# A 3x3 convolution with max pooling on one core: seven weight blocks turned by three transposes each, with a copied first tap, in a new program order

## The chip, the core and the metric

One core of a Trainium2 chip runs the whole kernel. The metric is the device time of one execution in microseconds (us); the time of a version is the median of several executions.

The engines: PE (TensorE) multiplies, PEld is its weight load, DVE (VectorE) and ACT (ScalarE) do element-wise work, POOL (GpSimd) does element-wise work and issues the converting loads, and SP (SyncE) issues the other transfers. Each engine works through a queue of its own in program order and waits at an instruction until the results it needs are there.

## The reference

```python
batch, c_in, h, w, c_out, k = 16, 64, 64, 64, 128, 3
x_pad = np.pad(x, ((0, 0), (0, 0), (1, 1), (1, 1)), mode='constant')
conv[b, co] += weight[co, ci, kh, kw] * x_pad[b, ci, kh:kh+h, kw:kw+w]   # over b, co, ci, kh, kw
output[b, c, i, j] = np.max(conv[b, c, 2*i:2*i+2, 2*j:2*j+2])
```

A convolution of 16 images with 64 channels of 64 x 64 to 128 channels, padded by one, and then the maximum over 2 x 2 squares. All of it is float32 on the outside; the kernel multiplies in bfloat16.

## The kernel before

**Tiles.** Two images lie together on the 128 partitions: image 0 of the pair on partitions 0 to 63, image 1 on 64 to 127. There are 8 pairs, each cut into 4 strips of 16 image rows, so 32 strips, numbered 0 to 31. A strip gives 8 rows of the output, and for each half h (image) two results of 8 x 64 numbers, one PSUM bank each: A for the odd and B for the even row of each pooled pair.

**Products.** A product (`product`, line 227) is three matmuls, one for each horizontal tap kw, on the 64 partitions of one image. The matmuls of h = 0 and h = 1 use different row halves of PE and are put into two lanes; the program takes one product from each lane and writes their matmuls in turn (lines 251 to 255). The text below calls this a pair. Strips of type "K" use the products PA1, PA2 into A and PB1, PB2 into B, straight from the image rows, and PR into B after a row maximum. Strips of type "W" use sums, differences and skip differences of neighbouring rows: P2, whose result is copied from A to B (`seed`, SE), P0 into A, P3 and P1 into B. In strip 0 the products are cut into halves a and b of four rows each.

**Weight blocks.** There are seven: G0, G1, G2 (the rows of the filter), D0 = G0 - G1, D2 = G2 - G1, GM and GP (half of G0 + G2 minus or plus G1; GS is the sum G0 + G2). Each is first made as `wq[m]`, 128 output channels on the partitions and 64 input channels for each tap along the row (`wcast` on ACT or `wpair` on DVE). Then PE turns it (`turn`, line 146): each transpose takes two neighbouring taps, 128 columns, so that one tap comes to the lower 64 partitions and the next one to the upper 64. `turn_out` (line 155) copies the turned block from PSUM to `wt[m]`. For h = 0 a matmul reads the lower half, for h = 1 the upper half (`tap_of`, line 135).

A block that isn't in `RING` (line 44) has its three taps between two slots of zeros (line 129) and needs four transposes. A block in `RING` has its three taps first and a copy of tap 0 behind them (`ring`, line 138, on POOL), and needs three.

**Row work.** Image rows 0 to 64 of pair 0 and 0 to 33 of pair 1 come as float32 through SP (line 89, six transfers) and are converted by `cast_rows` (CA on ACT, CV on DVE, line 100); all later rows are loaded and converted by transfers that POOL issues (`cload`, LK, line 94). `rows_op` (line 258) makes sums (S), differences (E) and skip differences (D): plain letters and a J run on DVE, a g on POOL. After the products: `evac` (EV, ACT) copies A out, `rowmax` (MX, DVE, line 294) takes the maximum of A and B into B, `odd` (OD, ACT, line 303) copies the odd columns, `colmax` (CM, DVE, line 316) takes the maximum with the even ones, and `store` follows on SP.

**Order.** The program order is written out by hand as a list of tokens, `ORDER` (line 326). Each token is one call; a number behind @ is the PSUM bank that the call takes. The queue of each engine is this list, cut down to the tokens of that engine. For example `uGM TGM@4` copies the first tap of GM, then turns the block into bank 4, and `VvGM` copies it out on DVE. Eight matmuls on constants (line 385) run before the list.

Of the kernel before, what the change touches and what calls it, by code (L numbers as in the profile page):

```python
# [10 lines left out]
def kernel(  # L11
# [123 lines left out]
    def tap_of(m, kw, h):  # L135
        return (kw - h) % K if m in RING or m == "GN" and "GM" in RING else kw + 1 - h

    def ring(m):
        behind_vector(nc.gpsimd.tensor_copy(out=wq[m][:, K, :], in_=wq[m][:, 0, :]))
# [173 lines left out]
    def colmax(part, s, h):  # L313
# [18 lines left out]
        EV.2.1 EV.1.0 MX.2.1 SE.1.1@4 PB1.2.0@2 LK.1.33.64.1 LK.2.0.33 Sg.3 MX.1.0 EV.2.0 OD.0.1 P0.1.1 P3.1.1
        CA.1.17.33 PR.2.1 EV.1.1 CM.0.1 OD.0.0 PB2.2.0 P2.3.0@7 EJ.4 P1.1.0 P2.3.1@3 SE.3.0@0 MX.1.1 OD.1.0
        OD.2.1 P1.1.1 P2.4.1@6 CM.0.0 Dg.5 LK.2.33.64 P0.3.0 LK.3.0.33 CM.1.0 SE.3.1@1 MX.2.0 P3.3.0 CM.2.1
        P0.3.1 PR.2.0 P3.3.1 OD.1.1 EV.3.0 SE.4.1@5 EV.3.1 P2.5.0@7 SE.5.0@3 CM.1.1 P2.4.0@4 D.4 P0.4.1 P0.5.0
        SJ.4 OD.2.0 LK.3.33.64 EV.4.1 MX.3.1 P3.4.1 MX.3.0 P2.5.1@6 P1.3.1 Dg.7 LK.4.0.33 CM.2.0 P3.5.0 EV.5.0
        SE.4.0@2 P1.3.0 SE.5.1@7 MX.4.1 LK.4.33.64 P1.4.1 P0.5.1 MX.5.0 P3.5.1 OD.3.0 P0.4.0 OD.3.1 EV.4.0 EJ.6
        OD.4.1 P3.4.0 CM.3.0 EV.5.1 P1.5.0 Dg.6 CM.3.1 MX.4.0 OD.5.0 P2.6.1@4 PA1.8.1@1 CM.4.1 P2.7.0@0 P1.4.0
        CM.5.0 SE.7.0@6 PA1.8.0@3 OD.4.0 SE.6.1@5 MX.5.1 PA2.8.1 EV.8.1 P0.7.0 P1.5.1 D.9 SJ.6 CM.4.0 P0.6.1
        OD.5.1 EV.7.0 LK.5.0.33 P3.7.0 PA2.8.0 P2.7.1@1 EV.6.1 P2.6.0@2 PB1.8.0@4 D.11 E.9 PB2.8.0 P3.6.1 CM.5.1  # L340
        SE.7.1@0 EJ.10 MX.6.1 EJ.12 EV.8.0 P0.7.1 SE.6.0@7 P2.9.1@3 EV.7.1 P1.6.1 P0.6.0 P3.7.1 P3.6.0 SE.9.1@1
        P0.9.1 OD.6.1 P2.11.1@2 LK.5.33.64 Sg.8 MX.7.0 P1.7.0 EV.6.0 MX.8.0 PR.8.0 CM.6.1 P3.9.1 MX.6.0 MX.7.1
        OD.7.0 P2.9.0@5 P1.7.1 EV.9.1 Dg.10 Sg.9 P1.6.0 OD.8.0 CM.7.0 CM.8.0 MX.9.1 SE.11.1@3 SE.9.0@6 P2.11.0@4
        OD.6.0 P0.11.1 CM.6.0 SJ.10 EJ.16 P3.11.1 OD.7.1 P0.9.0 EV.11.1 MX.11.1 CM.7.1 P2.10.1@2 Dg.12 SE.11.0@7
        P3.9.0 P1.9.1 P1.11.1 P0.11.0 EV.9.0 P3.11.0 MX.9.0 SE.10.1@5 P0.10.1 OD.9.1 PB1.8.1@1 CM.9.1 P2.12.0@0
        P1.9.0 P2.10.0@4 EV.11.0 P3.10.1 MX.11.0 OD.11.1 PB2.8.1 EV.10.1 OD.9.0 D.15 CM.11.1 SE.12.0@2 CM.9.0
        P1.11.0 SE.10.0@3 Dg.13 MX.10.1 P0.12.0 P2.12.1@6 OD.11.0 P0.10.0 P3.12.0 P1.10.1 EV.12.0 CM.11.0
        P3.10.0 SE.12.1@7 MX.8.1 P2.13.1@0 OD.10.1 P0.12.1 EV.10.0 P3.12.1 SJ.12 SE.13.1@4 CM.10.1 MX.12.0
        P0.13.1 P2.16.0@5 Dg.16 MX.10.0 EV.12.1 P1.12.0 SE.16.0@6 P3.13.1 PR.8.1 P1.10.0 OD.12.0 MX.12.1 CM.12.0
        OD.10.0 P0.16.0 CM.10.0 P1.12.1 EV.13.1 PA1.14.1@0 PA2.14.1 P2.13.0@2 PA1.14.0@3 OD.8.1 PA2.14.0 EV.16.0  # L350
        MX.13.1 SE.13.0@5 OD.12.1 P3.16.0 P0.13.0 Eg.15 Sg.15 CM.8.1 SJ.16 D.17 CM.12.1 P2.17.1@1 P1.13.1
        EV.14.0 EV.14.1 P2.15.0@7 SE.17.1@3 P2.15.1@0 P0.17.1 P3.17.1 OD.13.1 EV.13.0 SJ.18 P3.13.0 MX.16.0
        P1.16.0 PB1.14.1@4 SE.15.0@2 CM.13.1 P0.15.0 P3.15.0 EV.17.1 OD.16.0 SE.15.1@1 EJ.18 S.14 PB2.14.1
        MX.13.0 CM.16.0 P1.13.0 P0.15.1 EV.15.0 MX.17.1 PB1.14.0@6 P2.17.0@7 MX.15.0 MX.14.1 LK.6.0.33 OD.13.0
        P1.17.1 P3.15.1 CM.13.0 OD.17.1 EV.15.1 P1.15.0 SE.17.0@5 Dg.21 Sg.21 Dg.18 CM.17.1 MX.15.1 PB2.14.0
        PR.14.1 P2.16.1@0 OD.15.0 OD.14.1 Eg.21 CM.15.0 SE.16.1@3 MX.14.0 P1.15.1 P0.17.0 EV.17.0 P2.18.1@2
        OD.15.1 P3.17.0 CM.14.1 P0.16.1 PR.14.0 MX.17.0 SE.18.1@4 CM.15.1 EV.16.1 OD.14.0 P3.16.1 P2.18.0@7 D.19
        MX.16.1 LK.6.33.64 P1.17.0 P0.18.1 SE.18.0@1 P2.19.0@0 CM.14.0 P3.18.1 EV.18.1 OD.17.0 P0.18.0 P1.16.1
        LK.7.0.33 Dg.22 MX.18.1 CM.17.0 SE.19.0@6 P3.18.0 P2.21.1@2 P0.19.0 EV.18.0 P1.18.1 P2.19.1@7 MX.18.0
        OD.16.1 SE.21.1@5 P0.21.1 EJ.24 CM.16.1 P3.19.0 P1.18.0 EV.19.0 OD.18.1 SE.19.1@0 P3.21.1 Dg.25 P0.19.1  # L360
        LK.7.33.64 MX.19.0 EV.21.1 P2.21.0@3 OD.18.0 SE.21.0@2 P1.19.0 CM.18.1 EV.19.1 OD.19.0 PA1.20.0@4
# [98 lines left out]
```

## Time and profile before

| what | value |
|---|---|
| median of 3 runs | 103.37 us (102.65 to 103.5) |
| the profiled execution | 102.83 us, span 101.1 us, mean granted clock 0.994 |
| busy: PE, DVE, ACT, POOL | 94.8, 88.6, 85.4, 60.7 us |
| first product on PE | at 6.99 us of the span |
| moved by the transfers | 18.81 MB |

The span runs from the first to the last instruction; the profiled execution's time holds 1.7 us besides. In a row of the timeline stand the start, the duration from the first start to the last end of a merged group, the engine, the line, the operation and its shapes; behind a bracket, how long the engine was idle before it and what ended that. Rows of the chain are the stretches of work that led to the end, one after the other.

### The profile page before, as it was taken

Reading aid. Unit: us, or ns where it says so; the run is one execution under the profiler, and the core shown is the slowest. Engines: PE = TensorE matmul, PEld = TensorE weight load, DVE = VectorE, ACT = ScalarE, POOL = GpSimd, SP = SyncE. Lnnn points to the kernel's source line nnn. Section 1 sums busy time; section 2 is a strip of 40 time slices with the busy share of each in tenths; the row PEclk is TensorE's granted clock in tenths of the full one; section 3 lists DMA queues with packets and bytes.
Section 4 is the critical chain, followed back from the end, with each engine's and each line's share of the span. In section 5 each row is a group of like instructions: output and inputs, shape, how many; then the busy total and the mean of one; then the engine's idle time right before and its main releaser. Section 6 shows DMA issues by size and latency. Waiting matters only on the chain.

```text
span 101.1 us, 2423 instructions
## 1 busy us (share of the span) xinstructions
PE 94.8 (94%) x861; PEld 57.0 (56%) x861; DVE 88.6 (88%) x177; ACT 85.4 (85%) x188; POOL 60.7 (60%) x64
## 2 busy tenths in 40 slices
PE   6969999999999999999999999999999999999930
PEld 2349455548655656666666666676665555545300
DVE  0588999999999999999999999999976998969870
ACT  5540999999898999999988999899599989999830
POOL 7233486999606946798069995865994489600000
PEclk9999999999999999999999999999999999999997
DMA  2999649999999999993895159999925207332143
GB/s 74 270 359 412 266 47 178 195 237 221 226 230 228 229 232 225 304 334 135 98 192 182 62 65 218 206 264 218 292 99 179 73 6 242 122 113 98 52 150 109
DMA packets 11740, 18.81 MB, mean 186 GB/s; under 512 B 976, under 2 KB 9168, under 8 KB 11728
## 3 DMA queue, kind: packets, MB, share of 16 engines
q0 software_dynamic: 1872, 6.80, 36.6%
q1 hardware_dynamic: 9856, 11.87, 36.1%
q8 instruction: 6, 0.10, 0.4%
q14 instruction: 6, 0.05, 0.2%
HBM read 17.07 MB, written 8.39 MB: 252 GB/s over the span
## 4 chain that ended last, share of the span: by engine, by line
PE 79%; ACT 7%; DMA 5%; DVE 5%; issue 0%; SPq 0%; DVEq 0%
PE acc L242 78%; DMA xf<-in_x_dram 5%; ACT xb L100 3%; DVE xb L100 1%; DVE xf L316 1%; ACT acc L281 1%; ACT ev L289 1%; ACT od L303 1%; ACT ev L287 1%; DVE skip L272 1%; PE acc L149 0%; DVE dif L272 0%; SPq L106 0%; DVE wt_GP L161 0%; DVE sum L272 0%
## 5 line engine op out<-in xcount | busy, mean ns | idle before, releaser
L242 PE MATMUL acc<-skip,wt_G 64*128 64x504 bf16 (+1 forms) x312 | 65.7, 377 | 0.1
L242 PEld LDWEIGHTS <-wt_G 64*128 64x128 bf16 x432 | 34.8, 94 | 19.2 <-issue 2.6
L294 DVE TENSOR_TENSOR acc<-acc,ev 128x512 f32<-128x512 f32 x64 | 43.1, 693 | 2.0 <-ACT ev L287 1.5
L272 POOL TENSOR_TENSOR skip<-xb 128x1024 bf16<-128x1024 bf16 x17 | 36.0, 2126 | 11.0 <-DVE sum L272 4.6
L242 PE MATMUL acc<-dif,wt_GM 64*128 64x512 bf16 (+1 forms) x156 | 38.7, 376 | 0.0
L242 PE MATMUL acc<-sum,wt_GP 64*128 64x512 bf16 (+1 forms) x156 | 38.0, 377 | 0.2 <-DVE acc L294 0.2
L287 ACT ACTIVATE ev<-acc 128x512 f32<-128x512 f32 x52 | 31.3, 606 | 1.1 <-PE acc L242 0.8
L281 ACT COPY acc<-acc 128x512 f32<-128x512 f32 x52 | 30.5, 591 | 1.4 <-DVE xf L316 0.4
L303 ACT COPY od<-acc 128x256 f32<-128x256 f32 x64 | 23.3, 380 | 3.1 <-PE acc L242 2.8
L272 POOL TENSOR_TENSOR sum<-xb 128x512 bf16<-128x512 bf16 x10 | 11.5, 1150 | 12.3 <-DVE dif L272 4.5
L242 PEld LDWEIGHTS <-wt_GP 64*128 64x128 bf16 x156 | 14.2, 94 | 6.5 <-issue 1.2
L242 PE MATMUL acc<-xb,wt_D 64*128 64x504 bf16 (+3 forms) x84 | 16.6, 346 | 0.6 <-ACT xb L100 0.6
L242 PEld LDWEIGHTS <-wt_GM 64*128 64x128 bf16 x156 | 13.9, 94 | 5.5 <-ACT ev L287 0.3
L242 PE MATMUL acc<-xb,wt_G 64*128 64x504 bf16 (+6 forms) x84 | 16.0, 340 | 0.0
L316 DVE TENSOR_TENSOR xf<-acc,od 128x256 f32<-128x256 f32 x32 | 13.0, 418 | 2.2 <-ACT od L303 1.9
L316 DVE TENSOR_TENSOR o<-acc,od 128x256 f32<-128x256 f32 x32 | 13.1, 417 | 0.5 <-ACT od L303 0.3
L289 ACT COPY ev<-acc 128x512 f32<-128x512 f32 x12 | 6.9, 594 | 2.7 <-PE acc L242 2.6
L242 PE MATMUL acc<-sum,wt_G 64*128 64x504 bf16 (+1 forms) x36 | 8.9, 376 | 0.0
L242 PEld LDWEIGHTS <-wt_D 64*128 64x128 bf16 x84 | 6.5, 94 | 3.8 <-issue 1.2
L272 DVE TENSOR_TENSOR dif<-xb 128x1024 bf16<-128x1024 bf16 (+1 forms) x13 | 8.1, 622 | 0.1
L272 DVE TENSOR_TENSOR sum<-xb 128x1024 bf16<-128x1024 bf16 (+1 forms) x12 | 7.6, 638 | 0.0
L94 POOL DMA_DIRECT2D xb<-in_x_dram x13 | 7.5, 578 | 0.1
(37 smaller groups left out, 35.6 us busy)
## 6 DMA issues: line engine op xcount, KB each, us to landing
out_dram<-o SPq DMA_DIRECT2D x15, 256.0 KB, 9.4
xb<-in_x_dram POOLq DMA_DIRECT2D x7, 496.0 KB, 9.4
xb<-in_x_dram POOLq DMA_DIRECT2D x6, 528.0 KB, 8.9
out_dram<-xf SPq DMA_DIRECT2D x8, 256.0 KB, 6.0
out_dram<-xf SPq DMA_DIRECT2D x16, 128.0 KB, 1.9
xf<-in_x_dram SPq DMA_DIRECT2D x3, 512.0 KB, 6.7
xf<-in_x_dram SPq DMA_DIRECT2D x2, 544.0 KB, 6.7
xf<-in_x_dram SPq DMA_DIRECT2D x1, 480.0 KB, 7.4
```

What stands on the lines that cost most here:

```text
L94: inst = nc.gpsimd.dma_start(out=xb[p][:, lo + 1 : hi + 1, :], in_=rows_of(p, lo, hi))
L100: inst = nc.scalar.copy(out=dst, in_=src) if engine == "A" else nc.vector.tensor_copy(out=dst, in_=src)
L242: nc.tensor.matmul(t[:, i0:i1, o0:o1], wt[block][lo : lo + CI, tap_of(block, kw, h), :], rows(lo, i0, i1, c0, c1), start=start and kw == 1 ...
L272: inst = engine.tensor_tensor(out=dst, in0=in0, in1=in1, op=op)
L281: nc.scalar.copy(out=acc[home("B", part, s, h)][:, span, :], in_=acc[home("A", part, s, h)][:, span, :])
L287: nc.scalar.mul(dst, src, -1.0)
L289: nc.scalar.copy(out=dst, in_=src)
L294: nc.vector.tensor_tensor(out=t, in0=t, in1=ev[s % NEV, h][:, span, :], op=MAX)
L303: nc.scalar.copy(out=od[s % NEV, h][:, span, :], in_=acc[home("B", part, s, h)][:, span, 1::2])
L316: nc.vector.tensor_tensor(out=ot[s % len(ot)][:, h, i0:i1, :], in0=t[:, :, 0::2], in1=od[s % NEV, h][:, i0:i1, :], op=MAX)
```

## The change

All seven blocks are in `RING`, so each is turned by three transposes and none has slots of zeros any more. `ring` takes the engine that copies the first tap: a for ACT, v for DVE, anything else for POOL. The whole list `ORDER` is another one: the head of it is shown, of the rest the same kinds of calls stand in another order and with other banks, some of the row work on other engines (sums: six on DVE and six on POOL instead of two and ten, the ten J ones as before; differences: two and four instead of three and three; skip differences: eight and eighteen instead of nine and seventeen).

```diff
-    RING = ('G1', 'GM', 'GP')
+    RING = ('G0', 'G1', 'G2', 'D0', 'D2', 'GM', 'GP')
...
-    def ring(m):
-        behind_vector(nc.gpsimd.tensor_copy(out=wq[m][:, K, :], in_=wq[m][:, 0, :]))
+    def ring(m, engine):
+        dst, src = wq[m][:, K, :], wq[m][:, 0, :]
+        if engine == "a":
+            nc.scalar.copy(out=dst, in_=src)
+        elif engine == "v":
+            on_vector(nc.vector.tensor_copy(out=dst, in_=src))
+        else:
+            behind_vector(nc.gpsimd.tensor_copy(out=dst, in_=src))
...
-        D2 g1a g0a GS D0 TD2@0 TG0@1 GM GP VvD2 g2a CA.0.0.9 TG2@2 TD0@3 uGM TGM@4 PA1a.0.0@5 VvD0 VvG2
-        PA1a.0.1@6 uGP uG1 TG1@7 TGP@0 CV.0.9.17 PB1a.0.1@3 VvGP VaG0 PB1a.0.0@1 PB1b.0.0 PA1b.0.0 PB1b.0.1
-        PB2a.0.1 PB2b.0.0 PB2a.0.0 VvG1 VvGM PA2b.0.0 PA2a.0.0 Sg.0 PA2a.0.1 PA1b.0.1 PA2b.0.1 CV.0.17.33 E.1
-        S.1 CV.0.33.49 PB2b.0.1 EV.0.1 EV.0.0 P2.1.0@2 P2.1.1@0 SE.1.0@6 CA.0.49.64 PA1.2.1@4 PA1.2.0@7 D.1
...
+        D0 g0a GS uaG0 uvD0 g1a D2 uvG1 uvD2 g2a GM TG0@0 TD0@1 TG1@2 GP TD2@3 uaG2 uaGM TG2@4 VvD2 CV.0.0.9
+        VvG0 TGM@5 VaD0 uaGP CA.0.9.17 TGP@6 VaGP PB1a.0.1@1 PA1a.0.1@3 PA1a.0.0@7 PA1b.0.0 PA2b.0.0 PA2a.0.0
+        S.0 PB1a.0.0@0 PA2a.0.1 PA1b.0.1 PA2b.0.1 PB1b.0.1 VaG1 CV.0.17.33 VaG2 PB2a.0.1 PB2b.0.1 VaGM E.1 S.1
+        EV.0.0 PB1b.0.0 CV.0.33.49 P2.1.1@2 PA1.2.1@4 P2.1.0@6 PB2b.0.0 EV.0.1 PB2a.0.0 SE.1.0@7 PA2.2.1 D.1
+        CA.0.49.64 P0.1.0 MX.0.1 SE.1.1@3 EV.1.0 MX.0.0 P3.1.0 PR.0.0 EV.2.1 Sg.2 PB1.2.1@5 PB2.2.1 PA1.2.0@6
+        LK.1.33.64.1 S.3 CV.1.0.17 P0.1.1 LK.2.0.33 PR.0.1 P3.1.1 MX.1.0 Eg.3 OD.0.0 CA.1.17.33 PA2.2.0
+        PB1.2.0@4 CM.0.0 EV.1.1 MX.2.1 D.3 EJ.4 P2.3.0@0 EV.2.0 P2.3.1@2 P1.1.0 LK.2.33.64 Dg.5 PR.2.1 OD.0.1
+        MX.1.1 SE.3.0@6 PB2.2.0 CM.0.1 P1.1.1 P0.3.0 OD.1.0 SE.3.1@1 P3.3.0 OD.2.1 P0.3.1 CM.1.0 MX.2.0 EV.3.0
...
-            ring(name[1:])
+            ring(name[-2:], name[1])
```

In the token `uaGM` the second letter is the engine (a) and GM the block.

More of the change, by code (lines that the diff above doesn't have):

```diff
@@ L332 @@
[L332 to L361, printed above, removed]
@@ new lines @@
+        P1.5.0 OD.3.1 CM.3.0 OD.4.1 MX.4.0 OD.5.0 P2.7.0@6 CM.4.1 P2.6.1@3 CM.3.1 EV.5.1 P1.4.0 PA1.8.0@4
+        PA1.8.1@5 SE.7.0@1 CM.5.0 MX.5.1 PA2.8.1 Eg.9 Dg.6 OD.4.0 CM.4.0 P0.7.0 P1.5.1 SE.6.1@2 P2.7.1@7 PA2.8.0
+        P3.7.0 EV.8.1 D.9 S.8 SJ.6 P2.6.0@5 P0.6.1 PB1.8.0@0 EV.7.0 OD.5.1 CM.5.1 LK.4.0.33 LK.4.33.64 P3.6.1
+        SE.7.1@6 SJ.10 P0.7.1 LK.5.0.33 MX.7.0 EV.8.0 EV.6.1 SE.6.0@4 Sg.9 P2.9.1@3 P3.7.1 MX.6.1 EV.7.1 PB2.8.0
+        P0.6.0 SE.9.1@7 EJ.10 P1.6.1 MX.8.0 Dg.11 EV.6.0 P0.9.1 MX.7.1 P1.7.0 OD.6.1 OD.7.0 P3.6.0 P2.11.1@5
@@ new lines @@
+        EV.9.1 P1.7.1 PR.8.0 OD.8.0 SE.11.1@3 P3.9.1 CM.6.1 MX.6.0 P2.9.0@2 CM.7.0 P0.11.1 CM.8.0 OD.7.1 CM.7.1
+        SE.9.0@1 P1.6.0 P3.11.1 MX.9.1 Dg.10 OD.6.0 P2.11.0@0 P0.9.0 CM.6.0 EJ.12 SE.11.0@6 P3.9.0 EV.11.1
+        EV.9.0 P0.11.0 P3.11.0 P2.12.0@2 MX.11.1 P2.10.1@4 P1.9.1 SE.10.1@5 E.15 P1.11.1 LK.5.33.64 EV.11.0
+        MX.9.0 OD.9.1 OD.11.1 P1.9.0 MX.11.0 CM.9.1 CM.11.1 P0.10.1 P1.11.0 EV.10.1 P3.10.1 OD.9.0 MX.10.1
+        PB1.8.1@0 CM.9.0 SE.12.0@7 PB2.8.1 P2.12.1@3 Dg.12 EJ.16 LK.6.0.33 OD.11.0 P2.10.0@4 P0.12.0 P3.12.0
@@ new lines @@
+        P1.10.1 CM.11.0 SJ.12 D.13 SE.10.0@1 P0.10.0 P3.10.0 EV.12.0 SE.12.1@6 OD.10.1 P2.13.1@2 EV.10.0
+        SE.13.1@4 CM.10.1 P0.12.1 EV.12.1 P2.16.0@5 P3.12.1 SE.16.0@3 MX.12.0 MX.10.0 P0.13.1 MX.8.1 P1.12.0
+        MX.12.1 P3.13.1 P1.10.0 PR.8.1 Dg.16 P0.16.0 EV.13.1 Sg.15 LK.6.33.64 Dg.17 P2.13.0@2 OD.12.0 P1.12.1
+        P3.16.0 OD.10.0 MX.13.1 P1.13.1 OD.8.1 EV.16.0 CM.12.0 CM.10.0 CM.8.1 SE.13.0@7 OD.12.1 P2.17.1@1
+        PA1.14.0@5 P0.13.0 OD.13.1 MX.16.0 CM.12.1 PA1.14.1@0 PA2.14.0 P2.15.0@4 CM.13.1 SE.17.1@6 PA2.14.1
@@ new lines @@
+        P0.17.1 P3.17.1 SJ.16 D.15 P2.15.1@5 EV.13.0 EV.14.0 SE.15.0@2 EV.17.1 EV.14.1 P1.16.0 P3.13.0 P0.15.0
+        PB1.14.1@1 PB2.14.1 SJ.18 EJ.18 S.14 P3.15.0 MX.13.0 P1.13.0 SE.15.1@0 OD.16.0 MX.17.1 CM.16.0 P0.15.1
+        EV.15.0 OD.13.0 EV.15.1 Eg.21 P1.17.1 P3.15.1 Dg.21 PB1.14.0@4 OD.17.1 P2.17.0@3 P2.16.1@7 MX.15.0
+        SE.17.0@5 CM.13.0 P1.15.0 MX.14.1 OD.15.0 MX.15.1 Dg.18 CM.17.1 PB2.14.0 CM.15.0 P0.17.0 SE.16.1@6
+        PR.14.1 Dg.19 P1.15.1 OD.14.1 MX.14.0 EV.17.0 CM.14.1 P3.17.0 P2.18.1@2 MX.17.0 PR.14.0 SE.18.1@1
@@ new lines @@
+        OD.15.1 P0.16.1 Dg.23 EV.16.1 OD.14.0 P3.16.1 CM.15.1 P0.18.1 Sg.20 P3.18.1 P2.18.0@3 P1.17.0 MX.16.1
+        CM.14.0 SE.18.0@0 EV.18.1 P2.19.0@7 MX.18.1 P1.16.1 P0.18.0 SE.19.0@4 OD.17.0 CM.17.0 P2.21.1@2 P1.18.1
+        P3.18.0 OD.16.1 EV.18.0 P0.19.0 SE.21.1@5 P2.19.1@3 OD.18.1 P0.21.1 CM.16.1 MX.18.0 P3.19.0 CM.18.1
+        P3.21.1 SJ.22 EV.19.0 PA1.20.0@6 P2.21.0@1 SE.19.1@7 LK.7.0.33 Sg.21 P1.18.0 EV.21.1 P0.19.1 MX.19.0
+        P3.19.1 MX.21.1 P1.19.0 SE.21.0@2 P1.21.1 EJ.22 EV.19.1 P2.22.1@3 OD.19.0 OD.18.0 MX.19.1 P0.21.0
@@ new lines @@
+        CM.22.1 PA1.26.1@1 P2.22.0@4 PA2.26.1 OD.23.0 SE.22.0@7 P1.24.0 MX.25.1 P2.24.1@6 P1.25.1 OD.24.0
+        EV.26.1 PA1.26.0@3 P0.22.0 PA2.26.0 P3.22.0 SE.24.1@1 Dg.27 CM.24.0 CM.23.0 P2.23.1@2 EJ.28 SJ.28
+        EV.22.0 OD.25.1 PB1.26.0@4 P0.24.1 P2.27.0@0 SE.23.1@5 P3.24.1 EV.24.1 CM.25.1 EV.26.0 Sg.27 P0.23.1
+        P2.27.1@6 MX.22.0 MX.24.1 PB2.26.0 SE.27.0@3 P1.22.0 P0.27.0 P3.27.0 EJ.30 D.28 MX.26.0 EV.23.1
+        SE.27.1@2 Dg.29 PR.26.0 P3.23.1 P1.24.1 EV.27.0 OD.24.1 P0.27.1 P3.27.1 MX.23.1 OD.22.0 P2.29.0@0
@@ new lines @@
+        MX.27.0 CM.24.1 EV.27.1 P1.23.1 OD.26.0 CM.22.0 PB1.26.1@6 PB2.26.1 MX.27.1 OD.23.1 P1.27.0 CM.23.1
+        CM.26.0 P2.25.0@1 SE.29.0@7 MX.26.1 OD.27.0 CM.27.0 SE.25.0@5 P0.29.0 P1.27.1 P3.29.0 P0.25.0 P2.30.1@4
+        Dg.30 EV.29.0 P3.25.0 Dg.31 PR.26.1 OD.27.1 SE.30.1@3 CM.27.1 MX.29.0 EV.25.0 P2.29.1@0 OD.26.1 P0.30.1
+        P2.28.0@2 MX.25.0 CM.26.1 SE.29.1@1 P1.29.0 EV.30.1 P3.30.1 P0.29.1 SE.28.0@6 SJ.30 OD.29.0 P1.25.0
+        P2.31.1@4 P0.28.0 OD.25.0 EV.29.1 MX.30.1 CM.29.0 SE.31.1@7 EV.28.0 P1.30.1 P0.31.1 CM.25.0 P3.28.0
@@ L381 @@
+        P2.30.0@0 OD.30.1 P3.29.1 SE.30.0@5 EV.31.1 P2.31.0@2 MX.28.0 CM.30.1 P0.30.0 SE.31.0@3 MX.29.1 P3.30.0
+        P3.31.1 P0.31.0 EV.30.0 P2.28.1@4 P1.29.1 SE.28.1@0 P0.28.1 P3.28.1 MX.30.0 MX.31.1 OD.29.1 P3.31.0
+        CM.29.1 EV.31.0 P1.30.0 EV.28.1 P1.28.0 OD.30.0 MX.31.0 P1.31.1 P1.31.0 OD.31.1 OD.28.0 MX.28.1 CM.30.0
+        CM.31.1 P1.28.1 CM.28.0 OD.31.0 OD.28.1 CM.31.0 CM.28.1
     """
```

28 lines of the change are left out of this document (8 added, 20 removed).

## The prediction

> **What bounds the kernel now.** I read the page first (busy shares, then the chain that ended last), then the chain in order of time, then the timeline of the first 18 us engine by engine, and last the end of the run.
>
> ```profile
> PE 94.8 (94%) x861; PEld 57.0 (56%) x861; DVE 88.6 (88%) x177; ACT 85.4 (85%) x188; POOL 60.7 (60%) x64
> ...
> DVE  0588999999999999999999999999976998969870
> ```
> ```profile
> 6.99 0.50 PE acc L242 x6
> 7.50 0.46 PE acc L149 x6
> ...
> 20.71 74.94 PE acc L242 x683
> ```
> PE is the chain for 75 us without a break, so the stream of products is a floor: only its start, its holes and its tail can change. The products run in two lanes (image 0 on the lower 64 rows, image 1 on the upper), three taps of each lane in turn; I call that a pair. The holes are read from the starts of the pairs:
>
> ```profile
> 7.87 0.94 PE L242 MATMUL acc<-xb,wt_D 64*128 64x256 bf16 x13
> ...
> 10.10 0.81 PE L242 MATMUL acc<-dif,wt_GM 64*128 64x512 bf16 x6
> 10.92 0.82 PE L242 MATMUL acc<-xb,wt_D 64*128 64x512 bf16 x6
> 11.67 0.37 PE L242 MATMUL acc<-skip,wt_G 64*128 64x512 bf16 x1
> ...
> 13.61 0.83 PE L242 MATMUL acc<-sum,wt_G 64*128 64x512 bf16 x6
> 14.26 0.38 PE L242 MATMUL acc<-xb,wt_D 64*128 64x512 bf16 x1
> ...
> 16.46 0.62 ACT L281 COPY acc<-acc 128x512 f32<-128x512 f32 x1
> 16.47 0.69 DVE L294 TENSOR_TENSOR acc<-acc,ev 128x512 f32<-128x512 f32 x1
> ...
> 17.13 0.37 PE L242 MATMUL acc<-skip,wt_G 64*128 64x512 bf16 x1
> ```
> The four pairs from 11.67 to 14.26 take 2.59, 0.645 us each; a pair of half strips (parts a, b) takes half, with its start-up some 0.33. With that, the stream loses 0.55 us after its first pair (6.99 + 0.33 = 7.32, next at 7.87, the transposes of G1 and GP between), 0.175 before 10.92, 0.105 before 11.67 and 0.29 before 17.13 (four pairs from 14.26 end at 16.84), where P0 of strip 3 waits for its seed copy, begun at 16.46.
>
> **The prices that the head is worked out with.**
>
> ```profile
> 3.66 1.41 ACT L167 CAST wq_G<-wraw 128x192 bf16<-128x192 f32 x3 [1.64 <-DMA wraw<-in_weight_dram]
> 3.66 0.50 DVE L175 TENSOR_TENSOR wq_D<-wraw 128x192 bf16<-128x192 f32 x1 [3.66 <-DMA wraw<-in_weight_dram]
> ...
> 5.89 0.24 POOL L139 COPY wq_GM<-wq_GM 128x64 bf16<-128x64 bf16 x1 [2.82 <-DVE wq_GP L175]
> 6.27 0.67 ACT L100 CAST xb<-xf 128x576 bf16<-128x576 f32 x1 [1.21 <-DMA xf<-in_x_dram]
> 6.40 0.41 DVE L163 COPY wt_G<-acc 128x512 bf16<-128x512 bf16 x1
> 6.73 0.42 DVE L100 CAST xb<-xf 128x512 bf16<-128x512 f32 x1
> 8.52 0.35 DVE L161 TENSOR_SCALAR wt_GM<-acc 128x384 bf16<-128x384 bf16 x1
> 8.78 0.68 DVE L100 CAST xb<-xf 128x1024 bf16<-128x1024 f32 x1
> 9.50 0.43 DVE L272 TENSOR_TENSOR dif<-xb 128x512 bf16<-128x512 bf16 x1
> 10.06 1.07 ACT L289 COPY ev<-acc 128x512 f32<-128x512 f32 x2 [2.63 <-PE acc L242]
> 14.50 0.39 ACT L303 COPY od<-acc 128x256 f32<-128x256 f32 x1
> 14.76 1.08 ACT L100 CAST xb<-xf 128x1024 bf16<-128x1024 f32 x1
> ```
> Instructions overlap at their ends, so a queue moves by the distance of starts: on DVE 0.08 less than the duration (the turn-out at 6.40 lasts 0.41, the next starts at 6.73), on ACT 0.13 less (14.50 to 14.76 against 0.39). So DVE: 0.42 for a 192-wide pair operation, 0.33 for a 512-wide turn-out, 0.27 for a 384-wide one, 0.35 for a half-width sum or difference, 0.60 for a 1024-wide cast. ACT: 0.44 for a 192-wide cast ((1.41 - 0.13) / 3 is 0.43), 0.47 for a 512-wide copy ((1.07 - 0.13) / 2), 0.26 for a 256-wide one, some 0.95 ns an element in a cast of x.
>
> The 64-wide ring copy exists in this trace on POOL alone (0.24). On DVE, 128 columns less save 0.06, so 64 columns come to 0.27 - 0.15 = 0.12 at the low end and POOL's 0.24 is the high end; I take 0.12, the extrapolation on its own engine. On ACT, 256 columns less save 0.21, so 0.26 - 0.16 = 0.10 at the low end, and the 192-wide cast's 0.47 (1.41 / 3) is the high end; I take 0.12 of queue, with 0.25 until the result is seen. [...]
>
> **The change part by part.** *Removed:* four transposes (25 to 21), four memsets on POOL's head and three ring copies there, which nothing in the new head waits for; 128 columns from four turn-outs. *Added:* seven ring copies, three on DVE and four on ACT. *Moved:* all transposes stand ahead of the first product; five of the seven turn-outs run on ACT (one before), which sat idle for 1.21 and 2.63 us there (rows 6.27 and 10.06), so their 5 x 0.37 us is covered; the first cast of x goes to DVE, the second to ACT; the sum of strip 0 goes from POOL to DVE.
>
> The new head, walked from 3.66, where the weights are there:
> - DVE: D0, GS, ring D0, D2, ring G1, ring D2, GM, GP: 5 x 0.42 and 3 x 0.12, to 6.12; turn-out D2 to 6.39; cast of rows 0 to 9 (landed 6.25) to 6.74, seen at 6.83. Before, ACT's cast was seen at 6.95.
> - ACT: three casts and two copies by 5.3, ring GM when GM is seen (5.83), turn-out D0 to 6.31, ring GP to 6.43 (seen 6.52), cast of rows 9 to 17 to 6.95 (seen 7.04), then GP, G1, G2, GM out, the last seen at 8.57.
> - PE: the three GP transposes after 6.55, and the first products, PB1a and PA1a of strip 0, at 6.90.
>
> Behind them nothing in PE's queue waits for a transpose. Six half pairs end at 8.84 (row casts and G0 are there by 7.1). Strip 1's P2 needs its difference: DVE's strip-0 sum to 7.42, cast of rows 17 to 33 to 8.14, difference seen at 8.56; and GM out at 8.57. P0 of strip 1 starts at 10.46; its seed copy ends at 10.3 and its skip rows are seen at 10.12. Rows 33 to 49 are cast from 8.83; the transfers behind permit it:
>
> ```profile
> L89 SPq DMA_DIRECT2D xf<-in_x_dram x6: 417/438/901, 1.2 to 4.0; - x6
> ...
> DMA to landing us min/median/max: 5.1/7.0/8.7
> ```
> The first lands at 1.2 + 5.1 and the last at 4.0 + 8.7 = 12.7, six in a row, so about 1.3 us apart: 6.3, 7.5, 8.8, 10.1, 11.4, 12.7. Each cast in the new walk lies behind its landing by little: 0.05 to 0.3 us in the first three.
>
> One edit costs: in the new order P2.1.0 stands beside the half product PB2a.0.1, and PB2a.0.0 beside P2.1.1. Whether the short lane may run ahead is seen at the end of the run:
>
> ```profile
> 96.05 0.81 PE L242 MATMUL acc<-sum,wt_GP 64*128 64x512 bf16 x5 [0.19 <-DVE acc L294]
> ```
> Of the last six matmuls one started and five stood until 96.05, when lane 1's row maximum came: lane 0's other two taps waited behind lane 1's first. So matmuls start in order, and each mixed pair idles a lane for half a pair: together 0.33 us (bounds 0 and 0.33).
>
> The POOL queue: the load of strip 4's later rows (LK.1.33.64) waits for the cast of rows 49 to 64, which I put some 1.2 us earlier; strip 3's difference (Eg.3) now stands behind two such issues on POOL, to be seen at 13.85 against PE's need at 14.33. That is the tightest cover; without it P2.3.0 and all behind it in PE's order wait. The other twelve loads stay in their order on POOL and the stores on SP follow their column maxima.
>
> The sum: first product -0.09; hole behind it -0.55; holes before 10.92 and 11.67 -0.28; mixed pairs +0.33; the seed stall -0.29, since in the new order P0.3.0 stands two pairs further from P2.3.0 (its seed copy, 15.2 to 15.8 in the walk, is done before 16.27). Together -0.88. DVE, full from some 10 us until past 70 (its row of slices of 2.5 us), must be ahead too: its row maximum MX.1.1 (16.47, 0.69) was done at 17.1 and would be at 16.0, with strip 0's sum besides. For the rest I compared the two orders: 52 P2-to-P0 distances, seven of one pair before and five after (a sixth at one and a half); the last six column maxima and stores are the same. I count nothing for it, with +-0.4.
>
> 102.83 (the profiled execution, span 101.1 and 1.7 around it) - 0.88 = 101.95. That execution lay 0.54 under the median shown, 103.37, so against the median I forecast **102.5**, its own range 102.1 to 102.9.
>
> **The rivals.**
> 1. *The later holes go too: 101.8.* After 20.71 the old stream has 683 matmuls, 0.645 / 6 = 0.1075 each, 73.4 us, in 74.94: 1.5 us of holes, of which the new order might save half. For it: the engines that feed PE are 1.1 us ahead at 17 us. Against: two one-pair distances (P2.4.1 and P2.5.0 to their P0) stand near 18 us in the new order too.
> 2. *Given back: 103.2.* Either the ring copies cost their high ends (first product at 7.6, +0.7), or DVE, full until past 70 us, hands the lead back in the body. For it: DVE is nearly as full as PE. Against: by kinds its work falls by about 0.4 us.
> 3. *The new body waits: slower, 104.5.* P1 may start only after the row maximum that follows P0 and P3. The mean distance from them to P1 shrinks from 2.96 to 2.75 pairs, 0.135 us for each of 52 halves. It decides where DVE runs over 2.75 pairs (1.8 us) behind PE; if 60% of them wait the difference, 0.6 x 52 x 0.135 / 2 lanes = 2.1 us more than my sum, 102.5 + 2.1 = 104.6. Against it: two-pair distances are already common (22 before, 24 after) and PE stood full on them.
> 4. *The clock drops: 104.2.* Full products now end at 4.3 us and start at 6.90, with transposes alone between, as before.
>
> ```profile
> L385 PE MATMUL acc<-const-bfloat16-1.0 128*128 128x512 bf16 x8 | 3.6, 623 | 0.8 <-PEq L441 0.8
> ```
> ```profile
> 98.00:101.10 3.10, 0.00 (x0) 0.00 (x0) 0.00 (x0) 0.00 (x0) 0.00 (x0) 0.78 0.41 135
> ```
> The eight opening matmuls ran 0.43 us each, half the later speed, so warming took 3.5 us and costs 1.7 us of full work; and the granted clock fell to a half 2.9 us after the last product (0.78 mean over 98 to 101.1). The new gap of 2.6 us stays under that, and before's like gap kept 1.00; it decides if the ring copies cost their high end (7.6, a gap of 3.3). [...]
>
> **How the numbers follow.** Forecast 0.43; rival 1 0.22; rival 2 0.19; rival 3 0.13; rival 4 0.03. About 1% (1.03 us) is what a measurement here can tell from no change. Below 102.34 lie a third of the forecast (0.15) and rival 1: 0.37. Above 104.4 lie most of rivals 3 and 4: 0.12. Between: 0.51. The range 101.5 to 104.0 reaches over rivals 1 and 2 and leaves out most of 3 and 4.
>
> **What would show it.** Right: the first product at 6.8 to 7.1 and no hole of over 0.1 us until 8.8; full pairs at 10.4 and 16.3 for P0.1.0 and P0.3.0; two places near 9 us where one lane idles half a pair; DVE's 64-wide copy near 0.12 of queue. Wrong: a first product after 7.3, PE waiting on POOL's difference near 14 us, or a PE stream that is ahead at 17 us and not at 70.

## The result and the profile after

The changed kernel took 101.74 us (median of 4, 101.37 to 101.81) against 103.3 (median of 4, 102.65 to 103.5): a ratio of 0.9853 with an interval of 0.9804 to 0.9903. Run again beside other kernels it took 101.49 (median of 6) against 102.82: 0.985 (0.9814 to 0.9885). So it is faster by about 1.5% by the ratio, and by 1.3 to 1.6 us by the medians, where 102.5 us and a gain of 0.88 us were forecast. Comparisons use undisturbed executions alone, so a ratio can stand a little beside the quotient of the medians.

The profiled execution took 101.72 us, its span 100.0 (before 101.1). The page and the chain in order of time:

```profile
span 100.0 us, 2421 instructions
...
PE 94.3 (94%) x857; PEld 63.7 (64%) x857; DVE 88.0 (88%) x178; ACT 87.9 (88%) x196; POOL 58.5 (59%) x55
...
DVE  0599999999999999999999889989989998967960
```
```profile
9.96 0.61 DVE skip L278
10.57 0.05 issue
10.62 81.31 PE acc L248 x744
```
PE still sets the end, now unbroken from 10.62 instead of 20.71. The head engine by engine, in the timeline of the changed kernel:

```profile
4.24 0.24 ACT L141 COPY wq_G<-wq_G 128x64 bf16<-128x64 bf16 x1
4.39 0.96 ACT L173 CAST wq_G<-wraw 128x192 bf16<-128x192 f32 x2
5.00 0.18 DVE L143 COPY wq_G<-wq_G 128x64 bf16<-128x64 bf16 x1
5.12 0.18 DVE L143 COPY wq_D<-wq_D 128x64 bf16<-128x64 bf16 x1
5.22 0.50 DVE L181 TENSOR_TENSOR wq_GM<-gsum,wraw 128x192 bf16<-128x192 f32 x1
...
6.18 0.62 PE L155 MATMUL acc<-ident,wq_GP 128*128 128x128 bf16 x3
...
6.61 0.46 DVE L100 CAST xb<-xf 128x576 bf16<-128x576 f32 x1 [0.22 <-DMA xf<-in_x_dram]
...
7.12 0.83 PE L248 MATMUL acc<-xb,wt_D 64*128 64x256 bf16 x12 [0.32 <-DVE xb L100]
7.78 0.49 PE L248 MATMUL acc<-xb,wt_G 64*128 64x256 bf16 x6
...
9.07 0.37 PE L248 MATMUL acc<-dif,wt_GM 64*128 64x512 bf16 x1
9.08 0.39 PE L248 MATMUL acc<-xb,wt_G 64*128 64x256 bf16 x2
9.29 0.37 PE L248 MATMUL acc<-dif,wt_GM 64*128 64x504 bf16 x1
9.31 0.38 PE L248 MATMUL acc<-xb,wt_G 64*128 64x252 bf16 x2
...
9.97 0.57 ACT L287 COPY acc<-acc 128x512 f32<-128x512 f32 x1 [0.24 <-PE acc L248]
...
10.62 0.39 PE L248 MATMUL acc<-skip,wt_G 64*128 64x512 bf16 x1
```
The first 12 matmuls run without a break and the next six follow at 7.78: the hole of 0.55 us behind the first pair is gone. The first product came at 7.12, not 6.90, because the first rows of x landed at 6.59 (the cast at 6.61 stands behind 0.22 us of waiting for them), 0.34 later than before's 6.25. In the profile of the second run of the same kernel they landed at 5.87, and the walk's numbers come out:

```profile
6.33 0.45 DVE L100 CAST xb<-xf 128x576 bf16<-128x576 f32 x1
...
6.83 0.83 PE L248 MATMUL acc<-xb,wt_D 64*128 64x256 bf16 x12
...
94.56 0.81 PE L248 MATMUL acc<-sum,wt_GP 64*128 64x512 bf16 x5 [0.19 <-DVE acc L300]
```
The last line answers to the row at 96.05 in the prediction, the last pair; in the first profile of the changed kernel the same row starts at 94.94. From the start of the n-th pair in the order of time, before's minus the changed kernel's, one sees where the lead arises (us; the forecast sums the prediction's steps; the products in brackets are the changed kernel's):

| at | forecast | first profile | second profile |
|---|---|---|---|
| first product | 0.09 | -0.13 | 0.16 |
| second pair | 0.64 | 0.42 | 0.72 |
| tenth pair (P0.1.0) | 0.49 | 0.30 | 0.68 |
| 15th pair | 0.59 | 0.39 | 0.79 |
| 19th pair (P0.3.0) | 0.88 | 0.59 | 0.96 |
| 31st pair (near 24 us) | 0.88 | 0.73 | 1.10 |
| 49th pair | 0.88 | 1.07 | 1.45 |
| last pair | 0.88 | 1.11 | 1.49 |

Up to the 19th pair the second profile stays within 0.2 us of the forecast, and the first lies 0.2 to 0.3 under it, from the first product on, with its late landing. What the sum lacks is the 0.5 us gained from there to the 49th, some 36 us into the run: rival 1, with two thirds of the 0.75 us that it named.

The first product is no fair part of such a lead, since the landing differs from execution to execution. In e4 below, which has before's head, the first rows landed at 5.96:

```profile
6.71 0.51 PE L242 MATMUL acc<-xb,wt_D 64*128 64x256 bf16 x6 [0.18 <-ACT xb L100]
```
In e12, with the same head, they landed at 5.76 and the first product is at 6.50. Both times it is 0.74 or 0.75 behind the landing, as in before (6.25 and 6.99). The changed kernel starts at 6.83 with the rows there at 5.87, since its last transpose ends only at 6.82. So where the rows land before 6 us, the new head's first product is later than the old one's. The lead is made behind the first product: 1.24 and 1.33 us from there to the last pair, where the sum had 0.79.

### The profile page after: what moved, and what is told of

The parts are those of the page before. It is cut to its first block, busy times and chain, and to the rows that moved or that the text cites. A ratio compares the mean times of both kernels' runs of the same rounds, so it can differ in the third digit from the quotient of the medians.

```text
span 100.0 us, 2421 instructions
## 1 busy us (share of the span) xinstructions
PE 94.3 (94%) x857; PEld 63.7 (64%) x857; DVE 88.0 (88%) x178; ACT 87.9 (88%) x196; POOL 58.5 (59%) x55
## 4 chain that ended last, share of the span: by engine, by line
PE 82%; DMA 6%; DVE 6%; SPq 1%; issue 0%; ACT 0%; DVEq 0%
PE acc L248 82%; DMA xf<-in_x_dram 6%; DVE acc L300 3%; DVE xb L100 1%; DVE xf L322 1%; DVE skip L278 1%; DVE dif L278 0%; SPq L89 0%; ACT od L309 0%; SPq L106 0%; DVE sum L278 0%; DVEq L462 0%; DVEq L300 0%
## 5 line engine op out<-in xcount | busy, mean ns | idle before, releaser
L248 PE MATMUL acc<-skip,wt_G 64*128 64x504 bf16 (+1 forms) x312 | 64.2, 377 | 0.1
L248 PEld LDWEIGHTS <-wt_G 64*128 64x128 bf16 x432 | 36.8, 94 | 16.3 <-issue 2.0
L278 POOL TENSOR_TENSOR skip<-xb 128x1024 bf16<-128x1024 bf16 x18 | 38.0, 2126 | 11.5 <-PE acc L248 2.9
L248 PE MATMUL acc<-dif,wt_GM 64*128 64x512 bf16 (+1 forms) x156 | 39.9, 376 | 0.0
L248 PE MATMUL acc<-sum,wt_GP 64*128 64x512 bf16 (+1 forms) x156 | 37.2, 377 | 0.2 <-DVE acc L300 0.2
L248 PE MATMUL acc<-xb,wt_D 64*128 64x504 bf16 (+3 forms) x84 | 17.3, 346 | 0.3 <-DVE xb L100 0.3
L248 PE MATMUL acc<-xb,wt_G 64*128 64x504 bf16 (+7 forms) x84 | 17.5, 340 | 0.0
L278 POOL TENSOR_TENSOR sum<-xb 128x512 bf16<-128x512 bf16 x6 | 6.9, 1150 | 11.1 <-DVE skip L278 8.2
L248 PE MATMUL acc<-sum,wt_G 64*128 64x504 bf16 (+1 forms) x36 | 9.6, 377 | 0.0
L278 DVE TENSOR_TENSOR sum<-xb 128x1024 bf16<-128x1024 bf16 (+1 forms) x16 | 9.3, 589 | 0.0
```

The costliest lines, as they stand in the source:

```text
L248: nc.tensor.matmul(t[:, i0:i1, o0:o1], wt[block][lo : lo + CI, tap_of(block, kw, h), :], rows(lo, i0, i1, c0, c1), start=start and kw == 1 ...
L278: inst = engine.tensor_tensor(out=dst, in0=in0, in1=in1, op=op)
```

## The experiments

**Order alone and ring alone.** From the changed kernel, the four blocks go back to zero slots; and into the kernel before, all seven come into the ring, its order left.

```diff
 e1_order_only (from the changed kernel)
-    RING = ('G0', 'G1', 'G2', 'D0', 'D2', 'GM', 'GP')
+    RING = ('G1', 'GM', 'GP')
-  ... uaG0 uvD0 ... uvD2 ... uaG2
 e2_ring_only (from the kernel before)
+    RING = ('G0', 'G1', 'G2', 'D0', 'D2', 'GM', 'GP')
+  D2 uvD2 g1a g0a uaG0 GS D0 uvD0 ... g2a uaG2   (GM, GP, G1 copied on POOL)
```


> The new order with the old ring: G0, G2, D0 and D2 keep their zero slots and four transposes, and the four copies uaG0, uvD0, uaG2, uvD2 are left out; everything else as after. Theory 1 (the gain is in the order: fewer and shorter holes of PE, and the first product waits for the rows of x, not for the weights): the same as after within 0.3%, 0.983 to 0.988 of before, first product within 0.15 us of after's, the lead over before 1.0 us at the end of the stream. Rival (the three transposes and the copied tap carry the head): at least 0.4 us of the 1.5 us lost, 0.990 or more, with the first product 0.3 us later than in after.

> The old order with all seven blocks in the ring: copies of D2 and D0 on DVE, of G0 and G2 on ACT, each right behind its block; GM, GP and G1 copied on POOL as before. Theory 1: no gain, 0.997 to 1.004 of before, because the hole of 0.55 us behind the first pair comes from where the G1 and GP transposes stand, not from how many the others take; the two copies on DVE (0.12 each) come back as 0.06 less in each of three turn-outs. Rival: 0.990 to 0.995, with the hole shorter by 0.2 us or the first product earlier.

Measured: order alone 101.62 us against 102.67, ratio 0.9864 (0.9816 to 0.9911); ring alone 102.66, ratio 0.9971 (0.9937 to 1.0005). (Order alone also keeps the three copies of G1, GM and GP on DVE and ACT, where the kernel before has them on POOL.) The new order carries the gain, and the ring that the change is named after carries nothing that can be told from zero, though its interval reaches 0.6%. In the profile of order alone, with the rows of x landed at 5.97, the first product is at 7.06, 0.23 later than in the second profile of the changed kernel (6.83, landed at 5.87):

```profile
7.06 0.83 PE L248 MATMUL acc<-xb,wt_D 64*128 64x256 bf16 x12 [0.29 <-DVE xb L100]
```
So the ring may be worth up to 0.2 us in the head; the times don't show it (101.62 and 101.49).

**Head and body apart.** e3 has the first 145 tokens of the new list and then the old one; e4 the first 142 of the old list and then the new one (both cut near strip 5; banks renamed to fit).

> After's head (its first 145 tokens, up to about 24 us) with before's order for the rest, banks renamed to fit. Theory 1, that the parts add: after's lead at the 31st pair is 0.73 us and it gains 0.38 us behind it, so this one gains 0.73 us and keeps before's holes behind: 0.991 to 0.995 of before. Rival (a lead of the head is lost in the body because DVE is full there): 0.997 or more. Second rival (the head's lead alone also dissolves the later holes): 0.987 or less.

> Before's head (its first 142 tokens, up to about 24 us, weights with four and three transposes as before) with after's order for the rest, banks renamed. Theory 1: gains only the 0.38 us that after gains behind the 31st pair: 0.994 to 0.998 of before. Rival (the body needs the head's lead): 0.999 to 1.004. Second rival (the body alone makes the gain): 0.990 or less.

Measured: new head 102.07 us, ratio 0.9929 (0.9891 to 0.9967); new body 102.24, ratio 0.9945 (0.9904 to 0.9987). The product, 0.9929 x 0.9945 = 0.9874, is close to the whole change's 0.985: within these intervals the parts add. For the head this rests on the times alone, as the profiled execution of e3 took 102.98 us: there the fourth transfer of x landed at 11.13 (9.96 in before), and PE lost 0.9 us between the 11th and the 15th pair, where the products wait for work behind that transfer. In the profile with the new body, which has before's head, the lead over before is 0.29 at the first product, for the earlier landing, and still 0.29 at the 31st pair; it is 0.68 at the last:

```profile
95.37 0.81 PE L242 MATMUL acc<-sum,wt_GP 64*128 64x512 bf16 x5 [0.19 <-DVE acc L294]
```
That is 0.39 us behind the seam, the same 0.39 as between the 31st and the last pair in both profiles of the whole change (0.73 to 1.11, or 1.10 to 1.49). The order of the body, counted at nothing in the prediction, is a gain of its own.

**The changed kernel again.**

> The changed kernel unchanged, beside the others of this group. Theory 1 (holes): 0.988 to 0.992 of before, since before's median is 102.67 over more executions and the trace's lead is 1.1 us. Its first product comes at 6.8 to 6.9 where the first rows of x land by 6.3 us (7.12 at a landing of 6.59). Rival (the ratio of 0.985 first measured is the whole): 0.984 to 0.987.

Measured: 101.49 us, the ratio and profile given above. The first ratio stands, as the rival said, and 0.988 to 0.992 was too little; the first product came at 6.83 as expected.

**The hole behind the first pair.** The transposes of G1 and GP go back behind the first pair.

```diff
-  ... TD0@1 TG1@2 GP ... CA.0.9.17 TGP@6 VaGP PB1a.0.1@1 PA1a.0.1@3 PA1a.0.0@7 PA1b.0.0
+  ... TD0@1 GP ... CA.0.9.17 PB1a.0.1@1 PA1a.0.1@3 PA1a.0.0@7 TG1@2 TGP@6 VaGP PA1b.0.0
```


> After with the transposes of G1 and GP behind the first pair of products, as before had them, and GP's turn-out with them. The prediction counted 0.55 us for taking them out of there. Theory 1: a hole of 0.35 to 0.6 us behind the first pair is back (six transposes and the changeover), 0.003 to 0.006 slower than after, 0.993 to 0.997 of before. Rival (PE waits there anyway, for the row casts and turn-outs behind): the same as after within 0.1%.

Measured: 102.22 us, ratio 0.9957 (0.9917 to 0.9998). The matmuls at the start:

```profile
6.90 0.50 PE L248 MATMUL acc<-xb,wt_D 64*128 64x256 bf16 x6 [0.54 <-DVE xb L100]
7.33 0.34 PE L155 MATMUL acc<-ident,wq_G 128*128 128x128 bf16 x3
7.51 0.33 PE L155 MATMUL acc<-ident,wq_GP 128*128 128x128 bf16 x3
7.78 0.50 PE L248 MATMUL acc<-xb,wt_D 64*128 64x256 bf16 x6
```
From 6.90 + 0.33 the second pair could start at 7.23 and starts at 7.78: the hole of 0.55 is back, and the time is 0.7 us over the changed kernel's 101.49. The lead at the last pair is 0.72, half of the 1.49; beyond the hole, P2.1.0 waits longer (its start is 0.55 behind the pair before, where 0.33 is full speed). The largest term of the sum is confirmed by being undone.

**The ring copies twice.** Each copy is issued two times, to the same place.

```diff
+        for _ in range(2):
             if engine == "a":
                 nc.scalar.copy(out=dst, in_=src)
```


> After with each of the seven ring copies made twice (three more on DVE, four more on ACT). After's trace shows a copy at 0.10 to 0.15 us of queue on either engine. Theory 1 (the first product hangs on DVE's and ACT's weight work where the rows of x land early): the first product 0.3 to 0.45 us later than at the same landing in after, all of it kept to the end, 0.9900 to 0.9915 of before where after has 0.987, so 1.003 to 1.0045 of after. Rival (the copies lie beside the landing of x): the same as after within 0.1%. [...]

Measured: 103.43 us, ratio 1.0034 (0.9992 to 1.0077), and in the timeline of the head:

```profile
4.30 0.52 ACT L142 COPY wq_G<-wq_G 128x64 bf16<-128x64 bf16 x2
4.57 0.39 DVE L144 COPY wq_D<-wq_D 128x64 bf16<-128x64 bf16 x2
...
7.80 0.23 PE L156 MATMUL acc<-ident,wq_GP 128*128 128x128 bf16 x1 [0.46 <-ACT wq_GP L142]
7.97 0.86 PE L249 MATMUL acc<-xb,wt_D 64*128 64x256 bf16 x12
```
The first product is 1.14 us later than 6.83, and PE's last transpose before it waits for ACT's ring copy of GP. So the first product does hang on the copies, but the size missed by three times, and the profiled execution's 102.81 us is 1.5 over the 101.32 of the changed kernel's second one, where 0.3 to 0.45 was expected. A pair lasts 0.52 on ACT and 0.39 on DVE, about twice the single duration (0.24, 0.18): the second copy starts only when the first is done, which copies to different places don't (5.00 and 5.12 above). So doubling a short instruction on the same output prices its latency here, not its place in the queue.

**The mixed pairs.** The half products stand behind P2.1.1, so that halves run beside halves.

```diff
-  ... VaG2 PB2a.0.1 PB2b.0.1 VaGM ... P2.1.1@2 PA1.2.1@4
+  ... VaG2 VaGM ... P2.1.1@2 PB2a.0.1 PB2b.0.1 PA1.2.1@4
```


> After with the two mixed pairs undone: lane 1 runs P2.1.1 ahead of PB2a.0.1 and PB2b.0.1, so that P2.1.0 stands beside P2.1.1 and half products beside half products. Theory 1 (a lane without a wait runs ahead of the other; in after's trace the short lane started its second tap 0.09 us before the long one's): no gain, the same as after within 0.1%. Rival (the prediction's term: matmuls start strictly in order and each mixed pair idles a lane for half a pair): 0.33 us faster, 0.9965 to 0.9975 of after.

Measured: 101.52 us, ratio 0.9906 (0.9874 to 0.9938), against 0.985 (0.9814 to 0.9885) for the changed kernel in another group: no gain. The time alone would not settle it, as the wait of the next paragraph could hide up to 0.25 us of such a cost. The rows do: in the changed kernel's first profile half taps follow each other by 0.11 to 0.12 and full ones by 0.215 in both lanes, through both mixed pairs. They cost nothing.

**The hole before P0.1.0.** The changed kernel has a new hole at 10.62. Two kernels try to close it: e7 moves the skip difference D.1 ahead; e11 is to bring P2.1.0 and its seed copy forward, with strip 3's difference ahead of one load on POOL.

```diff
 e7_d_early
-  VaGM E.1 S.1 EV.0.0 PB1b.0.0 CV.0.33.49 P2.1.1@2 ... PA2.2.1 D.1 CA.0.49.64
+  VaGM E.1 D.1 EV.0.0 PB1b.0.0 CV.0.33.49 S.1 P2.1.1@2 ... PA2.2.1 CA.0.49.64
 e11_seed_early
-  PA2a.0.0 S.0 ... PB1b.0.1 VaG1 ... VaGM E.1 S.1 ... CV.0.33.49 ... PA2.2.1 D.1 ... LK.2.0.33 ... Eg.3
+  PA2a.0.0 ... PB1b.0.1 ... VaGM VaG1 E.1 S.0 ... CV.0.33.49 D.1 S.1 ... PA2.2.1 ... Eg.3 LK.2.0.33
```


> After with two moves on DVE: strip 1's skip difference D.1 right behind its difference E.1, and the sum S.1 behind the cast of rows 33 to 49. In after PE stood 0.25 us before P0.1.0 at 10.62, until D.1 was done at 10.57. Theory 1: that hole falls below 0.05 us and the end follows: 0.997 to 0.999 of after's time, 0.986 to 0.989 of before. Rival (the time is given back at the next wait, behind the row maxima on DVE): the same as after within 0.1%.

> After with five tokens moved, to bring P2.1.0 and with it the seed copy SE.1.0 forward: on DVE the sums S.0 and S.1 behind E.1 and D.1, D.1 behind the cast of rows 33 to 49, on ACT G1's turn-out behind GM's, on POOL strip 3's difference ahead of the load LK.2.0.33. The d-early kernel showed that the hole of 0.2 us before P0.1.0 is SE.1.0's (9.54 to 10.11, P0.1.0 at 10.16), not D.1's, done at 9.14. Theory 1: P2.1.0 starts 0.2 to 0.35 us earlier, the hole before P0.1.0 falls below 0.08 us, that before P2.3.0 (0.1) too, and the time falls to 0.996 to 0.998 of after's, 101.1 to 101.3 us. Rival (the time comes back at the next seed copies of the pairs 19 to 23): within 0.1% of after.

Measured: e7 101.34 us, ratio 0.9835 (0.98 to 0.9869); e11 101.5, ratio 0.9881 (0.9848 to 0.9913). Neither can be told from the changed kernel. In e7 the skip difference was done at 9.14 and the hole stayed; ACT's seed copy ends it:

```profile
9.54 0.57 ACT L287 COPY acc<-acc 128x512 f32<-128x512 f32 x1
```
```profile
8.46 0.68 DVE L278 TENSOR_TENSOR skip<-xb 128x1024 bf16<-128x1024 bf16 x1
```
The chain of the changed kernel names "DVE skip" for this wait, since it came last there (9.96 + 0.61) by 0.03 us; e7 shows that it isn't the cause. What e11 was to test it didn't: its P2.1.0 came no earlier (8.96, 2.05 behind the first product, against 1.95 and 1.89 in the changed kernel's profiles), since the second transfer of x landed at 7.65 and the cast and the difference stand behind it. But over the profiles P2.1.0 starts anywhere from 8.64 (e7) to 9.07, and the hole is 0.20 to 0.25 each time. The rows tell why: three taps of P2.1.0 take 0.81, the copy starts 0.09 later, lasts 0.57 and is seen 0.05 later, 1.52 in all (9.07 to 10.62 is 1.55, and it is 1.52 to 1.55 in nine profiles with this head); P2.1.0 itself and the two half products behind it in its lane, four times 0.32, fill 1.29. The hole is the difference of two fixed lengths. That it goes when one more half pair stands between was not tried.

**The stall of strip 3.** In the kernel before, P2.3.0 and its seed copy are moved ahead of OD.0.0 and PB2.2.0.

```diff
-  CM.0.1 OD.0.0 PB2.2.0 P2.3.0@7 EJ.4 P1.1.0 P2.3.1@3 SE.3.0@0 MX.1.1
+  CM.0.1 P2.3.0@7 SE.3.0@0 OD.0.0 PB2.2.0 EJ.4 P1.1.0 P2.3.1@3 MX.1.1
```


> Before with two tokens moved: P2.3.0 one product earlier in its lane, ahead of PB2.2.0, and its seed copy SE.3.0 ahead of OD.0.0 on ACT, so that two pairs instead of one lie between P2.3.0 and P0.3.0. Theory 1 (the hole of 0.29 us before P0.3.0 is the seed copy's, and after's order closes it by distance): the hole falls below 0.1 us and the stream stays that much ahead; 0.997 of before (0.9965 to 0.9985), where the interval will hardly tell it from 1 and the trace must. Rival (DVE, with MX.1.1 done at 17.1, holds P1.1.1 of the same pair at the same moment): the hole stays at 0.2 us or more and the time at that of before.

Measured: 103.09 us, ratio 1.0026 (0.9995 to 1.0057): no gain. In its timeline:

```profile
15.88 0.57 ACT L281 COPY acc<-acc 128x512 f32<-128x512 f32 x1
```
```profile
15.99 0.69 DVE L294 TENSOR_TENSOR acc<-acc,ev 128x512 f32<-128x512 f32 x1
```
```profile
16.51 0.37 PE L242 MATMUL acc<-skip,wt_G 64*128 64x512 bf16 x1
16.74 0.37 PE L242 MATMUL acc<-sum,wt_GP 64*128 64x512 bf16 x1
...
17.59 0.37 PE L242 MATMUL acc<-dif,wt_GM 64*128 64x512 bf16 x1
```
This execution ran 0.49 ahead of before from the first product on, for its landing. The seed copy is 0.58 earlier (15.88 for 16.46) and lane 0 gains 0.14 of its hole (a lead of 0.62 at the 19th pair), but lane 1's P1.1.1 at 16.74 still waits for the row maximum MX.1.1 (15.99 + 0.69 = 16.68), which gained nothing on the 0.49. Two waits stood at the same pair, and a third at the next: P2.4.1 starts at 17.59, when the second of two column maxima on DVE (16.78 + 0.76 = 17.54) is done. From the 24th pair on the lead is 0.35, less than at the start. In the changed kernel the seed copy and the row maximum are both earlier:

```profile
15.49 0.57 ACT L287 COPY acc<-acc 128x512 f32<-128x512 f32 x1
15.64 0.69 DVE L300 TENSOR_TENSOR acc<-acc,ev 128x512 f32<-128x512 f32 x1
...
16.55 0.38 PE L248 MATMUL acc<-skip,wt_G 64*128 64x512 bf16 x1
```

**Warm matmuls in the old head.** To see whether the gap ahead of the first product costs clock, the kernel before got two 512-wide matmuls on constants behind each of four transposed blocks (eight more on PE).

```diff
+  ... TD2@0 WARM.2 TG0@1 WARM.2 ... TD0@3 WARM.2 ... TGM@4 WARM.2
```


> Before with eight more matmuls on constants (512 wide, 128 rows), two each behind the transposes of D2, G0, D0 and GM, into a bank that is free there. The profile of the ring-only kernel showed PE's clock granted at half from 7.2 to 10.6 us, behind a stretch with little but transposes, at a cost of 1.5 us. [...] Rival (the drop has nothing to do with what PE does there): executions above 103.5 us stay as frequent as in before, about one in four. If the extra matmuls stand in the way, the median is up by 0.2 to 0.4 us.

Measured: 103.81 us, ratio 1.0074 (1.0046 to 1.0102), first product at 7.93:

```profile
4.76 1.06 PE L401 MATMUL acc<-const-bfloat16-1.0 128*128 128x512 bf16 x2
...
7.93 0.50 PE L242 MATMUL acc<-xb,wt_D 64*128 64x256 bf16 x6
```
The added matmuls stood in the way of the transposes: the 0.94 us by which the first product is late is still there at the last pair (0.97). So the run is slower for that and says nothing on the clock. It is inconclusive.

## Why the prediction was right and where it missed

**The number.** The range held the time, but 101.74 us is rival 1's 101.8 and not the forecast's 102.5. Part of the distance is the 0.54 us by which the forecast went from the profiled execution to a median: over 17 to 29 executions the kernel before has medians of 102.67 to 102.82, at its profile's 102.83, and the changed kernel's profile (101.72) lies at its median too. The other part is the sum: 0.88 forecast, 1.11 and 1.49 in the two profiles. That the sum fits up to P0.3.0 is partly luck, since a cost of 0.33 that was not paid stood against a new hole of 0.23 that was not foreseen.

**Right.** The stream of products is the floor, and a gain is a hole closed. The walk of the head put the first product at 6.90; it is 6.83 when the rows of x are there in time. (The 0.09 that the sum counts for it holds only against a landing at 6.25, as shown above.) The last GP transpose, put behind 6.55, starts at 6.57 (6.18 + 0.62 less its own 0.23). The hole behind the first pair went in full (e8). DVE's ring copies move the queue by 0.10 to 0.12 (5.00, 5.12, 5.22), the 0.12 taken; ACT's by 0.15 (4.24 to 4.39), a little over its 0.12. An ACT copy lasts 0.24, about the 0.25 taken until its result is seen, while the queue moves on after 0.15. So part of the duration is not queue time, nearly as taken, and rival 2's first half did not happen.

**The mixed pairs: +0.33, measured 0.** The step that failed. I read at the end of the run that one lane's taps waited behind the other's and made a rule of it. But there an instruction stood in a wait of 0.19 us for DVE's row maximum (the row at 96.05 in the prediction), and that held all behind it. Without a wait the lanes run independently here: in the rows from 9.07, lane 1 (xb, wt_G) starts two half taps from 9.08 (the second at 9.20) before lane 0's second tap at 9.29, although that one is ahead of it in the program. So in these rows PE's starts keep the order of its queue within a lane, not between the two.

**The holes before 10.92 and 11.67: -0.28, measured near -0.05 with the new hole.** The seed copy was right relative to its product: 8.84 to 10.3 in the walk, 8.72 to 10.19 in the second profile. But PE's need was put at 10.46, with the 0.33 of the mixed pairs in it. Without that, PE is there at 10.0 and waits 0.23 for the seed copy. The two errors are one: +0.33 not paid and 0.23 paid in its place. Over the two steps the lead was to fall by 0.05 from the second to the 15th pair, and went from 0.72 to 0.79 (0.42 to 0.39).

**The seed stall: -0.29, measured about that, with half of its cause missed.** The lead grows by 0.17 or 0.20 from the 15th to the 19th pair, with the new hole of 0.1 of the next paragraph in between. In the new order two pairs lie between P2.3.0 and P0.3.0 instead of one ("two pairs further" in the prediction). It named the seed copy for the pair at 17.13 and MX.1.1 only as a sign of DVE's lead; e12 shows that moving the copy alone gives nothing, as MX.1.1 holds the other lane and P2.4.1 waits in the next pair.

**The tightest cover missed by 0.1.** Strip 3's difference on POOL was to be seen at 13.85, with PE's need at 14.33:

```profile
13.39 1.16 POOL L278 TENSOR_TENSOR dif<-xb 128x512 bf16<-128x512 bf16 x1
...
14.60 0.37 PE L248 MATMUL acc<-dif,wt_GM 64*128 64x512 bf16 x1
```
It ended at 14.55 and PE started at 14.60, 0.085 late (its tap before started at 14.30, 0.215 each). The place was named rightly, with 0.7 us too little on POOL, and one of the prediction's own signs of being wrong, PE waiting there, did come, if small.

**The body: 0, measured -0.4 to -0.5.** This is the term that was mis-sized most, and it makes the forecast too high (-0.5 from the 19th pair on, -0.4 from the 31st). Counting one-pair distances (seven to five) says nothing of where they stand. In the kernel before, two of the holes are these, in two timelines:

```profile
28.80 0.57 ACT L281 COPY acc<-acc 128x512 f32<-128x512 f32 x1
...
29.42 0.37 PE L242 MATMUL acc<-skip,wt_G 64*128 64x512 bf16 x1
```
```profile
35.45 0.60 ACT L287 ACTIVATE ev<-acc 128x512 f32<-128x512 f32 x1
...
36.10 0.37 PE L242 MATMUL acc<-dif,wt_GM 64*128 64x512 bf16 x1
```
The first is P0.7.1, with one pair between P2.7.1 and it, waiting for its seed copy (28.80 + 0.57 = 29.37; hole 0.23). The second is P2.10.1, whose bank comes free with the evacuation at 35.45 (hole 0.2). In the new order P2.7.1 and P0.7.1 stand further apart, and P2.10.1 has another bank; its row in the changed kernel follows the pair before with 0.08:

```profile
35.06 0.37 PE L248 MATMUL acc<-dif,wt_GM 64*128 64x512 bf16 x1
```
That the body brings this gain is shown (e4). That it is these two holes was read from the traces; they were not undone one by one.

**Rivals.** Rival 3 (the new body waits) and rival 2's second half (the lead handed back) did not come: behind the 19th pair the lead never shrinks by more than 0.1 us, and DVE's row of slices has eights in it from the 23rd on (55 us), where before's has nines alone from the fifth to the 29th. The tail has the same stalls as before (0.19 ahead of the last pair). Rival 4 did not come either: the granted clock is 1.0 in both profiles.
